# Splitting the weights of a hybrid decoder step: 40 tiles ahead of time and w_o in the tail

## The chip, the cores and the metric

The kernel runs on one core of a Trainium2 chip. The metric is the device time of one execution in microseconds (us). A core has five engines that matter here, each working through its own instructions in order: TensorE (PE, matrix products), VectorE (DVE), ScalarE (ACT), GpSimd (POOL) and SyncE (SP, which here only issues transfers). A DMA transfer stands in the line of the engine that issues it: SP for what the code calls `load`, ACT for `store_`. If it has to wait for data or for a buffer, what stands behind it in that line waits too. SBUF is the core's working memory, PSUM the small memory that PE writes to (banks of 512 numbers for each of 128 partitions).

## The reference

One inference step of a decoder layer, for a prompt of 1024 rows and 64 sample rows, together T = 1088 rows of 1024 numbers, all in float32. In short:

```python
h = rmsnorm(x, norm_g) * (1 + scale) + shift              # from a small product of c
u_pool, z_pool, z_ssm, xbc, dt_raw, g_raw = split(h @ w_in)
p = (pool_mix(u_pool) * silu(z_pool)) @ w_pool_out        # 512 -> 1024
xbc = silu(causal_conv(xbc))                              # four taps
y = ssd(x, dt, A, B, C, state) + d_skip * x               # chunks of 128 rows, 32 heads
s = rmsnorm(y * silu(z_ssm), ssm_norm_g) @ w_ssm_out      # 2048 -> 1024
m = sigmoid(g_pool) * p + sigmoid(g_ssm) * s
x = x + gate * (m @ w_o)                                  # 1024 -> 1024, then a last rmsnorm
```

The layer also gives back new states of pooling, convolution and SSD.

## The kernel before

**Products in three parts.** PE multiplies numbers of reduced precision (`float32r`) at its fast rate. So each operand is split: `hi` is the operand rounded to float32r by a copy on ACT, `lo` the rest, `operand - hi`, by a subtraction on POOL or DVE. A product is hi x hi + hi x lo + lo x hi, three matmuls (lines 332 to 334 in `gemm_`, 492 to 494 in `product`). `split` (L160) does this for the tiles of w_in when they are needed: copy L163, subtraction L164.

**The main part** (some 90 to 660 us) is the projection h @ w_in. Its columns are taken in pairs of 128; a pair is one Strassen step of seven products (`strassen`, L498), each of two column blocks (24 matmuls). `run_units` (L1156) goes through a list of 22 such pairs, ones with a convolution or pooling behind them ("heavy") mixed with ones that only apply an activation (L559) and store ("light"), and two `gate_unit`s. At every `yield` of a pair it calls `beside()`, which here is one step of the generator `splits()`: seven steps per pair, one per gate unit, 156 in all. A convolution (`conv_unit`, L683) makes its four taps at L711 and L713, the activation at L716 and L717; it also copies 27 columns together (t27, L701) that PE transposes at L704 for the new state. `u_unit` (L594) does the same for the pooling state (u64, L615; PE at L618).

**`splits`** (L378) makes the hi and lo tiles of the other three weight matrices and puts them in DRAM, from where later parts load them. A job is a tile of 128 x 4 x 128: 8 of w_pool_out (to `wp_d`), 32 of w_ssm_out (to `ws_d`, each multiplied first by the norm's gain, four copies at L392), 16 of w_o (to `wo_d`). Each job loads to `pw` (L388, SP), yields, copies to `ph` (L394, ACT), subtracts in place (L396, POOL, every third job DVE), yields, stores both parts (L398 and L399, SP), and yields again in three jobs out of four. `pw` and `ph` have one buffer each, so that a load waits for the store before it. When the list is through, what is left of `splits` is run out in one go (L1223) and `to_ssd` (L1194) gives the memory to the next part and starts `dt_end` (L759).

**The samples** (to some 935 us). `dt_end` loads the raw dt from DRAM (L772 and L773, SP), transposes it on PE (L786), works out dt and the cumulated decays on DVE (L787 to L811) and so on. Beside nine more light pairs run the states of the sample rows (`ssd_samples`, L898).

**The chunks** (`chunk`, L1063) are the SSD over 8 chunks for 4 groups of heads, with the products of w_pool_out (`P_unit`) and of three groups of w_ssm_out (`S_unit`) between them in an order written out by hand for PE (`in_line`, L1146; the loop at L1335). A chunk's second step makes exponentials on ACT: cE (L1073), POOL masks (L868), eight heads (L877). `p_split` (L1128) loads the pooled rows (L1133), copies them to hi (L1137, ACT) and subtracts (L1138, DVE); P_unit needs them.

**The tail.** `tail_unit(m)` (L1427) multiplies with the last group of w_ssm_out; `m_done` (L1408) loads the stored gate (L1410) and the pooling part (L1413), multiplies the gate by 1/rms on POOL (L1411) and has DVE add, multiply, add (L1418, L1423, L1424); `m_split` (L1390) splits the result (L1404 ACT, L1405 DVE). `wo_prep` (L1381) loads hi and lo of a row block of w_o from `wo_d` (L1386 and L1387), for the samples' products (L1399) and the last product (L1515 to L1517).

**What sets the order.** The kernel is written as one stream of instructions; a scheduler with a timeline model of its own then orders the instructions of each engine, by their place in the stream as priority and by when it thinks that they can start. `tc.issue_after(i)` adds a compile-time edge: what the block traces on i's engine comes behind i on that engine. The line numbers below are those of the profile.

Of the kernel before, what the change touches and what calls it, by code (L numbers as in the profile page):

```python
# [8 lines left out]
F32 = mybir.dt.float32  # L9
# [21 lines left out]
P = 128  # L31
# [25 lines left out]
def tile_pool_ssd_step(  # L57
# [314 lines left out]

    wp_d = [dram(f"wp{m}", [P, 2, 4, P]) for m in range(8)]
    ws_d = [[dram(f"ws{g}{m}", [P, 2, 4, P]) for m in range(8)] for g in range(NG)]
    wo_d = [dram(f"wo{k}", [P, 2, D]) for k in range(8)]


    def splits():  # L378
        jobs = [(w_pool_out[0, :, m * P:(m + 1) * P].rearrange("(k p) c -> p k c", p=P), None, wp_d[m])
                for m in range(8)]  # L380
        jobs += [(w_ssm_out[0, g * 512:(g + 1) * 512, m * P:(m + 1) * P].rearrange("(k p) c -> p k c", p=P),
                  24 + 4 * g, ws_d[g][m]) for g in range(NG) for m in range(8)]
        jobs += [(w_o[0, k * P:(k + 1) * P, c * 512:c * 512 + 512].rearrange("p (k c) -> p k c", k=4), None,
                  wo_d[k][:, :, c * 512:c * 512 + 512].rearrange("p s (k c) -> p s k c", k=4))
                 for k in range(8) for c in range(2)]
        for n, (src, gain, dst) in enumerate(jobs):
            raw = small([P, 4, P], "pw", 1)
            load(raw, src)  # L388
            yield
            if gain is not None:  # L390
                for k in range(4):
                    act(raw[:, k], raw[:, k], AF.Copy, scale=vT[:, gain + k:gain + k + 1])  # L392
            hi = gas[0].tile([P, 4, P], F32R, tag="ph", name=nm("ph"), bufs=1)
            act(hi, raw, AF.Copy)  # L394
            lo = raw.bitcast(F32R)
            (V if n % 3 == 2 else nc.gpsimd).tensor_tensor(lo, raw, hi.bitcast(F32), ALU.subtract)  # L396
            yield
            load(dst[:, 0], hi.bitcast(F32))  # L398
            load(dst[:, 1], raw)  # L399
            if n % 4 < 3:  # L400
                yield

    def ready(d):
        def ws():
            with tc.high_priority(PRI):
                hi, lo = [wp.tile([P, 4, P], F32R, tag=t, name=nm(t), bufs=4) for t in ("whi", "wlo")]
# [187 lines left out]
    def u_unit(gi):  # L594
# [20 lines left out]
        nc.gpsimd.tensor_copy(u64, us[:, :, 15:23])  # L615
        ps = PB()
        nc.tensor.transpose(ps[:15, :P], up[:, SEQ:SEQ + 15], ident)
        nc.tensor.transpose(ps[:NS, P:2 * P], u64.rearrange("p b t -> p (b t)"), ident)  # L618
# [64 lines left out]
    def conv_unit(mc, dst):  # L683
# [17 lines left out]
        nc.gpsimd.tensor_copy(t27.rearrange("p (s t) -> p s t", t=3),  # L701
                              rp[:, SEQ:SEQ + 99].rearrange("p (s t) -> p s t", t=11)[:, :, 0:3])
        ps = PB()
        nc.tensor.transpose(ps[:27, :P], t27, ident)  # L704
        o27 = sm.tile([27, P], F32, tag="o27", name=nm("o27"))
# [22 lines left out]
    def gate_unit(half):  # L728
        c = slice(2 * D + half * 512, 2 * D + half * 512 + 512)

        def ws():
            out = []
            for j in range(4):
                w = GA([P, 2, 512])
                load(w, w_ada[0, 2 * j * P:(2 * j + 2) * P, c].rearrange("(k p) c -> p k c", p=P))
                out.append(w)
            return out

        def run(w):
            bg = gas[0].tile([P, 512], F32, tag="ph", name=nm("bg"), bufs=1)[:NB + 1]  # L740
            load(bg, b_ada[0, c].partition_broadcast(NB + 1))
            pg = PB()
            for kk in range(2):
                for r in range(4):
                    k = 4 * kk + r
                    mm(pg[32 * r:32 * r + 32, :], scT[:, k, :], w[k // 2][:, k % 2], start=(kk == 0), stop=(kk == 1))
            gs = pa.tile([P, 512], F32, tag="c2", name=nm("gs"))
            act(gs, pg, AF.Copy)
            yield
            ps = PB()  # L750
            mm(ps[:NB + 1, :], sel9, gs, start=True, stop=True)
# [376 lines left out]
    def p_split():  # L1128
        ph, pl = Y4(hs), Y4(hs)
        ph_.extend(ph[:, gi] for gi in range(4))  # L1130
        pl_.extend(pl[:, gi] for gi in range(4))
        for gi in range(4):
            load(pl[:, gi].bitcast(F32), yp_d[:, gi])  # L1133
        yield
        for gi in range(4):
            y = pl[:, gi].bitcast(F32)
            act(ph[:, gi], y, AF.Copy)  # L1137
            V.tensor_tensor(pl[:, gi], y, ph[:, gi].bitcast(F32), ALU.subtract)  # L1138
        yield
    ph_, pl_ = [], []  # L1140
    p_in = p_split()
# [191 lines left out]
            made += 1  # L1333

    in_line(True)  # L1335
    for i in (0, 1, 0):
        next(seq[i])
    for i in range(len(seq)):
        if i + 1 < len(seq):
            next(seq[i + 1])  # L1340
# [228 lines left out]
```

## Time and profile before

| | us |
|---|---|
| median of 3 runs (lowest, highest) | 1443.96 (1440.91, 1443.97) |
| the profiled execution | 1441.96 |
| its span, first to last instruction | 1440.2 |
| busy: PE, weight load (PEld) | 1299.5, 1182.2 |
| busy: DVE, ACT, POOL | 878.9, 704.4, 721.8 |
| mean granted clock of PE, share of full | 0.951 |

The profile is of one execution. A row of a group names line, engine, operation, output tile <- inputs and shape, then busy time and mean (ns), and the idle time of the engine just before, with what ended it. A row of waits reads "engine, what it ran next <- what ended the wait: us in total, times, longest". A row of a timeline is start, duration, engine, line and instruction; SPq and ACTq rows are issues of transfers. A row of stretches is start:end, length, busy time (and instructions) of PE, PEld, DVE, ACT and POOL, granted clock, share of the DMA engines' time, GB/s.

### The profile page before, as it was taken

To read this page: it belongs to the slowest core of one execution; us is meant where nothing else is said; L and a number is where in the kernel's file an instruction comes from. 1 tells how busy PE (TensorE), PEld (TensorE's weight loads), DVE (VectorE), ACT (ScalarE), POOL (GpSimd) and SP (SyncE) were. 2 spreads that over 40 slices of the span, in tenths; PEclk is the share of its full clock that TensorE was granted. 3 is DMA by queue.
4 is the path that set the end of the run, shared out by engine and by line. 5 is a ranking of instruction groups with operands and counts; after the bars stand their busy time and mean duration, and the time that the engine had idled before them with its cause. 6 is when DMAs were issued, how large, how long until landed. Compare 5 with 4: busy or idle time off the path is not lost. (4 is left out here: it accounts for less than half of the span.)

```text
span 1440.2 us, 26096 instructions
## 1 busy us (share of the span) xinstructions
PE 1299.5 (90%) x9545; PEld 1182.2 (82%) x9545; DVE 878.9 (61%) x1443; ACT 704.4 (49%) x1615; POOL 721.8 (50%) x629
## 2 busy tenths in 40 slices
PE   5898999889799898893699999969999999999998
PEld 2778899789799898893688889958888888998886
DVE  2875666465665673882456656537766677659543
ACT  3753355355454453442365455485678776501111
POOL 2375476576666674773345345314556564724000
PEclk8899999999899999997699999979999999999999
DMA  9235456454445445454355555477886665466431
GB/s 372 78 102 166 159 187 220 130 160 159 136 150 170 135 144 187 159 170 163 97 154 143 172 166 171 150 271 253 273 281 189 193 191 173 142 252 205 182 113 73
DMA packets 230522, 251.68 MB, mean 175 GB/s; under 512 B 31101, under 2 KB 173573, under 8 KB 230386
## 3 DMA queue, kind: packets, MB, share of 16 engines
q1 hardware_dynamic: 187444, 196.73, 42.6%
q10 hardware_dynamic: 42950, 53.28, 10.9%
q8 instruction: 76, 1.25, 0.4%
q14 instruction: 52, 0.43, 0.1%
HBM read 167.06 MB, written 83.01 MB: 174 GB/s over the span
## 5 line engine op out<-in xcount | busy, mean ns | idle before, releaser
L164 POOL TENSOR_TENSOR wlo<-raw,whi 128x512 fp32r<-128x512 f32 x128 | 195.9, 1535 | 180.3 <-ACT whi L163 162.0
L164 POOL TENSOR_TENSOR wlo<-rawA,whi 128x512 fp32r<-128x512 f32 x93 | 142.6, 1537 | 115.9 <-ACT whi L163 105.8
L332 PE MATMUL mm<-Y,whi 128*128 128x352 f32 (+3 forms) x504 | 174.1, 347 | 16.2 <-ACT Y L1137 10.4
L333 PE MATMUL mm<-Y,whi 128*128 128x352 f32 (+3 forms) x504 | 167.8, 333 | 4.2 <-DVE Y L281 2.3
L334 PE MATMUL mm<-Y,wlo 128*128 128x352 f32 (+3 forms) x504 | 166.4, 330 | 0.0
L492 PE MATMUL ps<-Y,whi 128*128 128x272 f32 x496 | 152.2, 307 | 2.9 <-ACT o L706 1.8
L492 PE MATMUL mm<-Y,whi 128*128 128x272 f32 x496 | 147.7, 298 | 3.2 <-ACT whi L163 3.2
L493 PE MATMUL ps<-Y,whi 128*128 128x272 f32 x496 | 149.1, 301 | 0.0
L494 PE MATMUL mm<-Y,wlo 128*128 128x272 f32 x496 | 146.8, 296 | 2.6 <-POOL wlo L164 2.6
L494 PE MATMUL ps<-Y,wlo 128*128 128x272 f32 x496 | 148.7, 300 | 0.0
L493 PE MATMUL mm<-Y,whi 128*128 128x272 f32 x496 | 145.4, 293 | 1.4 <-DVE Y L431 1.4
L713 DVE SCALAR_TENSOR_TENSOR GA<-GA,cvT,GA 128x1112 f32<-128x1112 f32 x72 | 129.4, 1812 | 27.5 <-ACT GA L711 27.5
L332 PEld LDWEIGHTS mm<-Y,whi 128*128 128x128 f32 x504 | 96.0, 191 | 25.5 <-ACT Y L1137 11.6
L163 ACT ACTIVATE whi<-raw 128x512 fp32r<-128x512 f32 x128 | 79.2, 622 | 67.0 <-PE ps L493 54.0
L492 PEld LDWEIGHTS ps<-Y,whi 128*128 128x128 f32 x496 | 99.7, 201 | 5.7 <-ACT o L706 2.0
L333 PEld LDWEIGHTS mm<-Y,whi 128*128 128x128 f32 x504 | 96.6, 192 | 7.3 <-DVE Y L1138 3.6
L492 PEld LDWEIGHTS mm<-Y,whi 128*128 128x128 f32 x496 | 95.4, 192 | 8.3 <-ACT whi L163 4.1
L392 ACT ACTIVATE pw<-pw,vT 128x128 f32<-128x128 f32 x128 | 41.1, 391 | 120.1 <-DMA pw<-in_w_ssm_out 108.9
L493 PEld LDWEIGHTS ps<-Y,whi 128*128 128x128 f32 x496 | 99.7, 201 | 0.0
L494 PEld LDWEIGHTS ps<-Y,wlo 128*128 128x128 f32 x496 | 99.6, 201 | 0.0
L494 PEld LDWEIGHTS mm<-Y,wlo 128*128 128x128 f32 x496 | 95.6, 193 | 4.1 <-POOL wlo L164 3.9
L493 PEld LDWEIGHTS mm<-Y,whi 128*128 128x128 f32 x496 | 95.6, 193 | 2.3 <-DVE Y L431 1.9
(406 smaller groups left out, 3804.9 us busy)
## 6 DMA issues: line engine op xcount, KB each, us to landing
rawA<-in_w_in SPq DMA_DIRECT2D x46, 512.0 KB
dec<-acs_d SPq DMA_DIRECT2D x32, 512.0 KB
xbc<-GA ACTq DMA_DIRECT2D x24, 512.0 KB
xb<-xbc SPq DMA_DIRECT2D x32, 384.0 KB
rawA<-in_w_in SPq DMA_DIRECT2D x32, 256.0 KB
pw<-in_w_ssm_out SPq DMA_DIRECT2D x32, 256.0 KB
ws<-ph SPq DMA_DIRECT2D x32, 256.0 KB
ws<-pw SPq DMA_DIRECT2D x32, 256.0 KB
```

The lines of the kernel that those rows point to most:

```text
L163: act(hi[:, :, :ncols], raw[:, :, :ncols], AF.Copy)
L164: nc.gpsimd.tensor_tensor(lo[:, :, :ncols], raw[:, :, :ncols], hi[:, :, :ncols].bitcast(F32), ALU.subtract)
L332: mm(ps[:, :n], a, rh[k][:, o:o + n], start=(k == 0), stop=False)
L333: mm(ps[:, :n], a, rl[k][:, o:o + n], start=False, stop=False)
L334: mm(ps[:, :n], b, rh[k][:, o:o + n], start=False, stop=(k == nk - 1))
L392: act(raw[:, k], raw[:, k], AF.Copy, scale=vT[:, gain + k:gain + k + 1])
L492: mm(p, hi, ah, start=(k == 0), stop=False)
L493: mm(p, hi, al, start=False, stop=False)
L494: mm(p, lo, ah, start=False, stop=(k == 3))
L713: V.scalar_tensor_tensor(d[:, :n], rp[:, k:k + n], cvT[:, 24 * k + mc:24 * k + mc + 1], d[:, :n], ALU.mult, ALU.add)
```

## The change

- `splits` keeps 40 jobs; the 16 of w_o and the tensors `wo_d` go.
- A job's steps are spread: load; one step, or two in three jobs of four; gain, copy and the store of hi; a step later the store of lo; another step. The stores are issued by ACT, not SP. The block with ACT's instructions is traced under `behind(Activation)`: they come behind the last ACT instruction traced so far. All subtractions are POOL's.
- `wo_prep` loads w_o itself, copies to hi on ACT and subtracts on POOL, tile by tile in the tail.
- t27 and u64 are copied by ACT, not POOL. Two of the four subtractions of `p_split` go to POOL. `gate_unit` takes a buffer of the large kind.
- Ahead of the chunk loop the exponential steps of the first two chunks come behind the last ACT instruction traced so far.

```diff
-    wo_d = [dram(f"wo{k}", [P, 2, D]) for k in range(8)]
+    def behind(engine):
+        return tc.issue_after(next(i for i in reversed(nc.cur_bb.bb.instructions) if i.engine == engine))
...
-        jobs += [(w_o[0, k * P:(k + 1) * P, c * 512:c * 512 + 512].rearrange("p (k c) -> p k c", k=4), None,
-                  wo_d[k][:, :, c * 512:c * 512 + 512].rearrange("p s (k c) -> p s k c", k=4))
-                 for k in range(8) for c in range(2)]
         for n, (src, gain, dst) in enumerate(jobs):
-            raw = small([P, 4, P], "pw", 1)
-            load(raw, src)
+            raw = gas[0].tile([P, 4, P], F32, tag="pw", name=nm("pw"), bufs=1)
+            load(raw, src.rearrange("(k p) c -> p k c", p=P))
             yield
-            if gain is not None:
-                for k in range(4):
-                    act(raw[:, k], raw[:, k], AF.Copy, scale=vT[:, gain + k:gain + k + 1])
+            if n % 4:
+                yield
             hi = gas[0].tile([P, 4, P], F32R, tag="ph", name=nm("ph"), bufs=1)
-            act(hi, raw, AF.Copy)
-            lo = raw.bitcast(F32R)
-            (V if n % 3 == 2 else nc.gpsimd).tensor_tensor(lo, raw, hi.bitcast(F32), ALU.subtract)
+            with behind(mybir.EngineType.Activation):
+                if gain is not None:
+                    for k in range(4):
+                        act(raw[:, k], raw[:, k], AF.Copy, scale=vT[:, gain + k:gain + k + 1])
+                act(hi, raw, AF.Copy)
+                store_(dst[:, 0], hi.bitcast(F32))
+            nc.gpsimd.tensor_tensor(raw.bitcast(F32R), raw, hi.bitcast(F32), ALU.subtract)
             yield
-            load(dst[:, 0], hi.bitcast(F32))
-            load(dst[:, 1], raw)
-            if n % 4 < 3:
-                yield
+            with behind(mybir.EngineType.Activation):
+                store_(dst[:, 1], raw)
+            yield
...
-        nc.gpsimd.tensor_copy(u64, us[:, :, 15:23])
+        act(u64, us[:, :, 15:23], AF.Copy)
...
-        nc.gpsimd.tensor_copy(t27.rearrange("p (s t) -> p s t", t=3),
-                              rp[:, SEQ:SEQ + 99].rearrange("p (s t) -> p s t", t=11)[:, :, 0:3])
+        act(t27.rearrange("p (s t) -> p s t", t=3),
+                              rp[:, SEQ:SEQ + 99].rearrange("p (s t) -> p s t", t=11)[:, :, 0:3], AF.Copy)
...
-            bg = gas[0].tile([P, 512], F32, tag="ph", name=nm("bg"), bufs=1)[:NB + 1]
+            bg = GA([P, 512])[:NB + 1]
...
-            V.tensor_tensor(pl[:, gi], y, ph[:, gi].bitcast(F32), ALU.subtract)
+            (nc.gpsimd if gi % 2 else V).tensor_tensor(pl[:, gi], y, ph[:, gi].bitcast(F32), ALU.subtract)
...
-    for i in (0, 1, 0):
-        next(seq[i])
+    with behind(mybir.EngineType.Activation):
+        for i in (0, 1):
+            next(seq[i])
+    next(seq[0])
...
-        load(hi.bitcast(F32), wo_d[k][:, 0])
-        load(lo.bitcast(F32), wo_d[k][:, 1])
+        raw = M((P, D))
+        load(raw, w_o[0, k * P:(k + 1) * P, :])
+        act(hi, raw, AF.Copy)
+        nc.gpsimd.tensor_tensor(lo, raw, hi.bitcast(F32), ALU.subtract)
         wo[k] = (hi, lo)
```

More of the change, by code (lines that the diff above doesn't have):

```diff
@@ L374, in tile_pool_ssd_step @@
     ws_d = [[dram(f"ws{g}{m}", [P, 2, 4, P]) for m in range(8)] for g in range(NG)]
-    wo_d = [dram(f"wo{k}", [P, 2, D]) for k in range(8)]
+    def behind(engine):
+        return tc.issue_after(next(i for i in reversed(nc.cur_bb.bb.instructions) if i.engine == engine))
     def splits():
[L379 to L382, printed above, removed]
-        jobs += [(w_o[0, k * P:(k + 1) * P, c * 512:c * 512 + 512].rearrange("p (k c) -> p k c", k=4), None,
-                  wo_d[k][:, :, c * 512:c * 512 + 512].rearrange("p s (k c) -> p s k c", k=4))
-                 for k in range(8) for c in range(2)]
+        jobs = [(w_pool_out[0, :, m * P:(m + 1) * P], None, wp_d[m]) for m in range(8)]
+        jobs += [(w_ssm_out[0, g * 512:(g + 1) * 512, m * P:(m + 1) * P], 24 + 4 * g, ws_d[g][m])
+                 for g in range(NG) for m in range(8)]
@@ L403, in ready, with wtiles @@
+            nc.gpsimd.tensor_tensor(raw.bitcast(F32R), raw, hi.bitcast(F32), ALU.subtract)
+            yield
+            with behind(mybir.EngineType.Activation):
+                store_(dst[:, 1], raw)
+            yield
+    def wtiles():
+        return [wp.tile([P, 4, P], F32R, tag=t, name=nm(t), bufs=4) for t in ("whi", "wlo")]
     def ready(d):
@@ L405, in ws @@
             with tc.high_priority(PRI):
-                hi, lo = [wp.tile([P, 4, P], F32R, tag=t, name=nm(t), bufs=4) for t in ("whi", "wlo")]
+                hi, lo = wtiles()
                 load(hi.bitcast(F32), d[:, 0])
```

## The prediction

> **What bounds the kernel now.** I read the page first, for where TensorE (PE) is not busy.
>
> ```profile
> span 1440.2 us, 26096 instructions
> ...
> PE   5898999889799898893699999969999999999998
> ...
> ACT  3753355355454453442365455485678776501111
> ...
> PEclk8899999999899999997699999979999999999999
> ```
>
> Each digit is 36 us. PE is nearly full from slice 27 (972 us) on, and there are two holes before it: slices 18 and 19 (the seam from the projection to the sample states, here the first seam) and slice 26 (the seam to the chunks, the second). The stretches say how full PE is after the second seam and in the tail:
>
> ```profile
> 972.00:1260.00 288.00, 284.80 (x2266) 252.86 (x2265) 200.33 (x279) 198.38 (x546) 160.49 (x192) 0.99 0.67 212
> 1260.00:1332.00 72.00, 67.60 (x386) 63.60 (x385) 52.59 (x59) 7.73 (x13) 24.21 (x10) 1.00 0.67 229
> ```
>
> The columns are length, then busy time of PE, weight load, DVE, ACT, POOL, then clock. With PE busy 284.8 of 288 us, a microsecond that PE gains ahead of 972 us reaches the end. So the list of what PE waited for is a list of prices:
>
> ```profile
> PE ps L786 <- DMA s<-dts_d: 30.2, 1, 30.2
> ...
> PE ps L704 <- POOL t L701: 15.9, 6, 5.1
> ...
> PE mm L332 <- ACT Y L1137: 10.4, 3, 5.9
> ...
> PE ps L618 <- POOL u L615: 6.2, 2, 4.8
> ...
> PE mm L333 <- DVE Y L1138: 1.9, 3, 0.6
> ```
>
> Total, number and longest of the waits. The change touches all five. The longest of them begins at 693.25 - 30.19 = 663.06 us by PE's timeline:
>
> ```profile
> 693.25 1.12 PE L786 MATMUL ps<-ident,s 128*128 128x128 f32 x4 [30.19 <-DMA s<-dts_d]
> ```
>
> **The first seam, a wait removed.** Twelve-microsecond stretches around the 30.2 us:
>
> ```profile
> 648.00:660.00 12.00, 10.92 (x85) 10.48 (x84) 5.29 (x10) 6.41 (x15) 8.93 (x7) 1.00 0.77 266
> 660.00:672.00 12.00, 1.74 (x12) 1.55 (x12) 2.34 (x6) 1.90 (x4) 1.39 (x2) 0.71 0.26 98
> 672.00:684.00 12.00, 0.00 (x0) 0.00 (x0) 0.89 (x4) 0.63 (x1) 1.26 (x1) 0.50 0.36 126
> 684.00:696.00 12.00, 2.75 (x13) 2.76 (x14) 1.54 (x4) 0.63 (x1) 3.96 (x13) 0.50 0.37 114
> 696.00:708.00 12.00, 12.00 (x87) 11.95 (x87) 9.39 (x17) 7.19 (x12) 6.47 (x5) 0.87 0.34 106
> 708.00:720.00 12.00, 9.08 (x43) 7.64 (x41) 5.60 (x16) 5.26 (x9) 1.85 (x2) 0.72 0.23 72
> ```
>
> No engine is busy there: it is a chain of latencies. SyncE's (SP's) timeline shows which:
>
> ```profile
> 682.20 0.33 SPq L388 DMA_DIRECT2D pw<-in_w_o  x1
> ...
> 685.62 0.32 SPq L398 DMA_DIRECT2D wo<-ph  x1
> ...
> 686.96 0.32 SPq L399 DMA_DIRECT2D wo<-pw  x1
> ...
> 689.44 0.32 SPq L772 DMA_DIRECT2D s<-dts_d  x1
> ```
>
> This is the last split of w_o: load, copy, subtract, two stores, one buffer, so that each takes some 7 us end to end (682.20 to 689.44). The load of dt that PE's transposes of L786 need stands behind it on SP and issues 2.5 us after its last store. Leftover splits run one by one between 664 and 689 us. How late the splits are is in the rows of their tile:
>
> ```profile
> L388 SPq DMA_DIRECT2D pw<-in_w_ssm_out x32: 367/383/396, 186.5 to 539.4; - x32
> ...
> L388 SPq DMA_DIRECT2D pw<-in_w_o x16: 328/333/341, 556.0 to 682.2; - x16
> ...
> L388 SPq DMA_DIRECT2D pw<-in_w_pool_out x8: 383/390/498, 89.5 to 160.0; - x8
> ```
>
> The main part gives 22 pairs x 7 + 2 = 156 steps from 89.5 to about 663 us, 3.7 us each. 56 jobs of 2.75 steps ask for a job every 10.1 us; the middle row makes one each (539.4 - 186.5) / 31 = 11.4 us. So they fall behind and the rest spills over. After the change 40 jobs of 3.75 steps take 150 steps: 13.8 us each, above the 11.4 that the chain needs, and the last one ends near 89.5 + 150 x 3.7 = 645 us, some 18 us before PE's last product. The 16 jobs of w_o are gone. What is late next is dt's load itself, 3.8 us from issue (689.44) to PE's start (693.25), which can now run beside the last products. I take 28 of the 30.2 us; the ends are 0 (splits still late) and 30.2.
>
> The clock was 0.50 in the hole and 0.87 and 0.72 in the 24 us behind it: 12.0 x 0.13 + 9.08 x 0.28 = 4.1 us of PE work at most. In part PE waits there for the dt arithmetic anyway (9.08 of 12 busy), so I take 2 us.
>
> **The second seam, an order changed.** ScalarE's (ACT's) timeline with one row of the chain that ended last, and then two rows of the tail, for the price of such a subtraction on POOL (the group of L1411) and on DVE:
>
> ```profile
> 650.84 0.43 ACT L559 ACTIVATE u<-u 128x272 f32<-128x272 f32 x1 [0.40 <-ACT s L559]
> ...
> 939.95 10.50 DMA Y<-yp
> ...
> 949.13 1.28 ACT L1073 ACT_TABLE_LOAD   x1
> ...
> 956.89 1.09 ACT L1137 ACTIVATE Y<-Y 128x1088 fp32r<-128x1088 f32 x1
> ...
> 961.03 2.15 ACT L877 ACTIVATE dec<-dec,acT 128x128 f32<-128x128 f32 x7
> ...
> 967.44 1.09 ACT L1137 ACTIVATE Y<-Y 128x1088 fp32r<-128x1088 f32 x1
> ...
> L1411 POOL TENSOR_TENSOR R<-R,sq_acc 128x1088 f32<-128x1088 f32 x8 | 22.2, 2787 | 52.5 <-issue 32.9 <-DMA R<-gs 13.4 <-DVE m L1405 5.0
> ...
> 1302.07 1.28 DVE L1423 TENSOR_TENSOR G<-G,R 128x1088 f32<-128x1088 f32 x1
> ```
>
> The pooled rows have landed at 950.4, but the four copies of L1137 run between 956.89 and 968.5, mixed with exponentials of the first two chunks and with the sigmoids of L559; each swap of function loads a table (1.28 us). The pins put the exponentials behind the last sigmoid traced: four copies (4.4 us) and about five sigmoids (0.43 each, 2.1) could then be done near 957 in place of 968.5. The exponentials that follow (one table, 16 of about 0.3, cE) take some 7 us, to 964, when they also end now. Against that, two of four subtractions of L1138 go to POOL, 2.8 us for such a tile where DVE takes 1.3. Of 10.4 + 1.9 = 12.3 us I take 8; ends 0 and 12.3.
>
> [...]
>
> **The main part, work moved.** POOL's copies of t27 and u64 go to ACT, the stores of the splits from SP to ACT, and all 40 subtractions to POOL (before, 38 there and 18 on DVE).
>
> ```profile
> L701 POOL COPY t<-GA 128x27 f32<-128x27 f32 x24 | 12.0, 530 | 0.0
> ...
> L396 DVE TENSOR_TENSOR pw<-pw,ph 128x512 fp32r<-128x512 f32 x18 | 19.6, 1091 | 50.9 <-ACT ph L394 50.9
> ...
> ACT pw L392 <- DMA pw<-in_w_ssm_out: 108.9, 24, 8.4
> ...
> ACT ph L394 <- DMA pw<-in_w_o: 56.3, 13, 7.2
> ...
> SPq L399 <- POOL pw L396: 53.2, 36, 7.4
> ```
>
> PE's 15.9 + 6.2 = 22.1 us are waits for small copies that stand behind subtractions on POOL. On ACT, too, each should be a copy of no more than the 0.53 us that it takes on POOL. ACT has its own stalls, 108.9 + 56.3 us for loads of splits: the first shrinks, since the copies now come one or two steps (3.7 to 7.4 us) after the load and are pinned there; the second goes. I take 14 of the 22.1; ends 0 and 22.1.
>
> What is added: 40 pairs of stores stand in ACT's line. A store of ACT's own result costs a gap of 0.40 us (the row of L559 above): 40 x 0.4 = 16 us. The second store waits for POOL: SP waited 53.2 us in 36 such cases, 1.5 us each and 7.4 at worst, which for 40 is 59 us. Behind it on ACT stand the copies into whi (POOL and then PE's weights wait for them), the copies of L516 (DVE and PSUM banks) and the activations of the convolution. But the store is traced one step of 3.7 us after the subtraction, so that only the long waits show. I take 6 us on PE's path; ends 0 and 75. DVE loses 19.6 us of work and POOL 12.0 less 2 subtractions; PE is not counted as gaining from it, ACT's and PE's own work being the cover. At nothing too: gate_unit's buffer, and the 16 MB less that go out and back for w_o (no row of PE's waits names them).
>
> **The tail, work added.** Per row block of w_o: one 512 KB load in place of two, a copy on ACT (about 1 us; ACT is busy 7.73 of 72 us) and a subtraction of 128x1024 on POOL (2.6 us, from the 2.79 of L1411 by its columns). POOL has the time; DVE hasn't, and is held up by it:
>
> ```profile
> 1307.09 2.83 POOL L1411 TENSOR_TENSOR R<-R,sq_acc 128x1088 f32<-128x1088 f32 x1 [6.59 <-DMA R<-gs]
> ...
> 1308.05 3.02 DVE L1423 TENSOR_TENSOR G<-G,R 128x1088 f32<-128x1088 f32 x1
> ```
>
> The same DVE instruction takes 1.28 us alone (the row at 1302.07 above) and 3.02 beside POOL: it ends 1.15 us after POOL does, so it hardly ran before. In the tail DVE leads (chain of L1418, L1423, L1424, L1405) and PE follows closely. Five subtractions inside the units at 3.02 - 1.28 = 1.74 us are 8.7; the last three come in line after the seventh unit (w_o's last buffers come free only then), 2.6 us each, of which PE's partial sums hide some: 3.3. I take 12. The lower end is 0 (some run in POOL's idle stretch ahead of the tail, up to 32.9 us long by the group's row), the upper 8 x 2.6 = 21, all on the path.
>
> [...]
>
> **Sum.** -28 - 2 - 8 - 14 + 6 + 12 = -34 us. The profiled execution took 1441.96 us (span 1440.2 and 1.8 around it): 1408. The median of the runs is 2.0 above that: 1410.
>
> **Rivals.**
> 1. *The tail locks DVE out in full* (21 in place of 12) and the small copies gain only half (-7): 1410 + 9 + 7 = 1426. For it, the rows of L1423; against it, POOL's idle time ahead of the tail.
> 2. *The splits are still late.* If a job takes over 13.8 us (ACT reaches a copy late, the store waits, the next load waits for the store), a few jobs spill over again and dt's load stays behind them: the 28 us stay and the time is 1438. For it, four waits per job across four engines; against it, the 11.4 us measured and 18 us of slack at the end.
> 3. *Slower: ACT becomes the jam.* ACT waits at the second store for POOL, and whi, L516 and the convolution wait behind it. The price at most 75 us, less the 6 taken: 1410 + 69 = 1479. It decides from 34 us on the path, 0.85 us per job. For it, SP's 53.2 us of just this wait, on a queue where less stood behind it; against it, ACT is busy some half of this part (mostly digits 3 to 5 on the page), the wait comes a step later, and 165 us of ACT's older stalls shrink.
> 4. *It doesn't do what it says*: the scheduler puts the leftover elsewhere on the path, and nothing changes: 1444.
>
> **Chances.** Forecast (1394 to 1424) 0.68, rival 1 0.12, rival 2 0.08, rival 3 0.09, rival 4 0.03. A measurement here tells about 0.2% (2.9 us) from no change. Faster 0.88, same 0.03, slower 0.09. Range 1394 to 1434: low by both seams and the copies in full with a cheap tail, high to between rivals 1 and 2.
>
> **What would show it.** The wait of L786 under 5 us and a clock near 1 from 660 to 720: the first seam right; over 20: rival 2. L1137's copies in one row ahead of L877's exponentials, PE's wait there under 5: the second. ACT's waits for POOL's pw over 30 us, and PE waiting for whi and L516: rival 3. L1423 and L1424 near 3 us beside POOL's new subtraction, and the stretch from 1290 to 1350 longer by over 15 us after shifting: rival 1. I would be wrong altogether if PE found as much to wait for between 100 and 660 us as it lost.

## The result, and the profile after

The changed kernel takes 1382.43 us (median of 4 runs, 1380.84 to 1384.85), the kernel before 1443.62 us beside it (4 runs, 1440.91 to 1443.97): a ratio of 0.958, interval 0.956 to 0.960. The forecast was 1410 us, its range 1394 to 1434. The profiled execution took 1383.51 us, its span is 1381.8.

Page of the kernel after, the same lines as of before; PE's hole at slices 18 and 19 (digits 3 and 6 before) is gone, the one of the second seam is still there (8 and 7 at slices 25 and 26, counted from 0):

```profile
span 1381.8 us, 25855 instructions
...
PE   5899899898899999998999999879999999988998
...
ACT  3854355455455555554644554367688766121311
PEclk9899999999999999999999999979999999999999
```

Lines move by about four: L786 is L790, L704 is L708, L618 is L622, L394 is L396. PE's waits after:

```profile
PE ps L708 <- ACT t L705: 11.3, 6, 4.2
...
PE ps L622 <- ACT u L619: 6.2, 3, 2.5
...
PE ps L790 <- DMA s<-dts_d: 4.3, 1, 4.3
```

The wait for dt fell from 30.2 to 4.3 us. But the small copies, forecast to give 14 of their 22.1 us, still cost 11.3 + 6.2 = 17.5: ACT's now, not POOL's. The time came from elsewhere, as a comparison at the same work shows. A pair is 168 matmuls, so the start of a pair is found by counting. Pairs are numbered from 0 in PE's order, so that the 22 of the main part are 0 to 21 and 22 is the first beside the samples; a stretch runs from the start of one pair to the start of the other:

| stretch of the same work | before | after | difference | forecast |
|---|---|---|---|---|
| pairs 1 to 22 | 541.3 | 510.4 | -30.9 | -14 + 6 |
| first seam (pair 22 to 23) | 63.5 | 32.9 | -30.6 | -28 - 2 |
| sample states (pair 23 to 30) | 214.6 | 213.0 | -1.6 | 0 |
| second seam (pair 30 to the first product of L1105, now L1109) | 46.4 | 43.0 | -3.4 | -8 |
| chunks | 304.4 | 305.8 | +1.4 | 0 |
| tail | 160.4 | 166.3 | +5.9 | +12 |

With 0.8 us ahead of pair 1 that is the difference of the two spans, 58.4 us. The first row is the miss. Its stretches in the kernel before, cut at pairs 12 and 16 (length, then busy time of PE, weight load, DVE, ACT, POOL, then clock):

```profile
109.70:399.20 289.50, 261.87 (x1933) 248.97 (x1931) 177.66 (x280) 133.47 (x298) 186.62 (x132) 0.95 0.51 165
399.20:498.60 99.40, 91.72 (x689) 89.08 (x689) 61.64 (x101) 51.29 (x119) 67.75 (x47) 0.97 0.47 151
498.60:651.00 152.40, 137.75 (x1034) 134.54 (x1033) 105.43 (x148) 69.22 (x148) 104.58 (x73) 0.96 0.50 166
sum 541.30, PE 491.34 PEld 472.59 DVE 344.73 ACT 253.99 POOL 358.95; mean PE 163.78 PEld 157.53 DVE 114.91 ACT 84.66 POOL 119.65
```

And in the kernel after:

```profile
110.50:389.70 279.20, 256.74 (x1932) 244.35 (x1930) 176.33 (x272) 129.44 (x290) 181.87 (x121) 0.97 0.50 158
389.70:482.90 93.20, 88.32 (x690) 86.38 (x690) 60.47 (x97) 49.65 (x117) 67.05 (x43) 1.00 0.48 152
482.90:620.90 138.00, 132.05 (x1033) 129.24 (x1032) 97.33 (x139) 75.19 (x172) 98.94 (x65) 1.00 0.46 151
sum 510.40, PE 477.11 PEld 459.97 DVE 334.13 ACT 254.28 POOL 347.85; mean PE 159.04 PEld 153.32 DVE 111.38 ACT 84.76 POOL 115.95
```

PE stood still for 541.3 - 491.3 = 50.0 us before and 33.3 after, 16.7 less; and the same products took 477.1 us of busy time in place of 491.3, 14.2 less, at a higher clock.

What ACT waits for says where to look. Before, beside the 108.9 and 56.3 us of the prediction, there is a row for the first eight jobs; the other two rows are of after:

```profile
ACT ph L394 <- DMA pw<-in_w_pool_out: 22.8, 5, 7.1
```

```profile
ACT pw L395 <- DMA pw<-in_w_ssm_out: 80.2, 23, 6.6
...
ACT ph L396 <- DMA pw<-in_w_pool_out: 8.5, 4, 3.8
```

So the time in which ACT stands at a split's load, with what it would do for PE behind it, fell from 188 us to 88.7. In the kernel before, part of it stood behind the rows that name POOL. This is PE's second longest wait for a small copy, in the lines of ACT, POOL and PE:

```profile
135.27 0.63 ACT L394 ACTIVATE ph<-pw 128x512 fp32r<-128x512 f32 x1 [7.14 <-DMA pw<-in_w_pool_out]
```

```profile
135.98 1.27 POOL L396 TENSOR_TENSOR pw<-pw,ph 128x512 fp32r<-128x512 f32 x1 [4.64 <-ACT ph L394]
```

```profile
137.48 0.42 PE L618 MATMUL ps<-ident,u 128*64 128x128 f32 x1 [4.84 <-POOL u L615]
```

PE waits for POOL's copy, which stands behind a subtraction of `splits`; the subtraction waits for ACT, and ACT for the load. In the three longest of these waits (5.12, 4.84 and 3.26 us, together 13.2 of the 22.1) POOL had stood idle for 4.3 to 4.7 us for a split's copy on ACT, and ACT for 5.8 to 7.1 us ahead of that copy, in two of the three for its load by name. In the other five POOL was at work on the lo tiles of w_in (L164).

One such case in the kernel after, on three engines, first ACT:

```profile
357.00 0.33 ACTq L401 DMA_DIRECT2D ws<-pw  x1
...
365.18 1.28 ACT L395 ACTIVATE pw<-pw,vT 128x128 f32<-128x128 f32 x4 [6.59 <-DMA pw<-in_w_ssm_out]
366.36 0.21 ACT L705 ACTIVATE t<-GA 128x27 f32<-128x27 f32 x1
```

then SP, then PE:

```profile
362.24 0.37 SPq L387 DMA_DIRECT2D pw<-in_w_ssm_out  x1
```

```profile
366.63 0.41 PE L708 MATMUL ps<-ident,t 128*27 128x128 f32 x1 [4.16 <-ACT t L705]
```

The second store of a split is issued at 357.00. The next load has the same buffer and is issued only at 362.24, when that store has landed; over all jobs SP stood 180.1 us for this:

```profile
SPq L387 <- DMA ws<-pw: 180.1, 29, 12.3
```

The load lands at 365.18; ACT, which came to the copy 6.59 us before that, goes on, does the small copy at 366.36, and PE, which has waited for 4.16 us, transposes it. The row of waits says "ACT t"; the cause is two transfers in one buffer.

### The profile page after: what moved, and what is told of

The parts are those of the page before. It is cut to its first block, busy times and chain, and to the rows that moved or that the text cites. A ratio compares the mean times of both kernels' runs of the same rounds, so it can differ in the third digit from the quotient of the medians.

```text
span 1381.8 us, 25855 instructions
## 1 busy us (share of the span) xinstructions
PE 1284.0 (93%) x9545; PEld 1171.3 (85%) x9545; DVE 874.7 (63%) x1423; ACT 696.6 (50%) x1625; POOL 733.1 (53%) x613
## 5 line engine op out<-in xcount | busy, mean ns | idle before, releaser
L164 POOL TENSOR_TENSOR wlo<-raw,whi 128x512 fp32r<-128x512 f32 x128 | 182.3, 1428 | 174.9 <-ACT whi L163 150.6
L164 POOL TENSOR_TENSOR wlo<-rawA,whi 128x512 fp32r<-128x512 f32 x93 | 142.2, 1532 | 99.6 <-ACT whi L163 93.5
L717 DVE SCALAR_TENSOR_TENSOR GA<-GA,cvT,GA 128x1112 f32<-128x1112 f32 x72 | 134.0, 1876 | 30.4 <-ACT GA L715 29.2
L496 PE MATMUL ps<-Y,whi 128*128 128x272 f32 x496 | 147.0, 296 | 2.0 <-ACT o L710 2.0
L498 PE MATMUL mm<-Y,wlo 128*128 128x272 f32 x496 | 145.7, 294 | 0.9 <-POOL wlo L164 0.8
L497 PE MATMUL ps<-Y,whi 128*128 128x272 f32 x496 | 144.2, 291 | 0.0
L498 PE MATMUL ps<-Y,wlo 128*128 128x272 f32 x496 | 143.6, 289 | 0.0
L496 PEld LDWEIGHTS ps<-Y,whi 128*128 128x128 f32 x496 | 94.9, 191 | 4.3 <-ACT o L710 2.3
L334 PEld LDWEIGHTS mm<-Y,wlo 128*128 128x128 f32 x504 | 97.8, 194 | 0.3
L498 PEld LDWEIGHTS mm<-Y,wlo 128*128 128x128 f32 x496 | 94.9, 191 | 1.9 <-POOL wlo L164 1.5
L497 PEld LDWEIGHTS ps<-Y,whi 128*128 128x128 f32 x496 | 94.7, 191 | 0.0
L498 PEld LDWEIGHTS ps<-Y,wlo 128*128 128x128 f32 x496 | 94.6, 191 | 0.0
```

The source lines that it names most:

```text
L164: nc.gpsimd.tensor_tensor(lo[:, :, :ncols], raw[:, :, :ncols], hi[:, :, :ncols].bitcast(F32), ALU.subtract)
L334: mm(ps[:, :n], b, rh[k][:, o:o + n], start=False, stop=(k == nk - 1))
L496: mm(p, hi, ah, start=(k == 0), stop=False)
L497: mm(p, hi, al, start=False, stop=False)
L498: mm(p, lo, ah, start=False, stop=(k == 3))
L717: V.scalar_tensor_tensor(d[:, :n], rp[:, k:k + n], cvT[:, 24 * k + mc:24 * k + mc + 1], d[:, :n], ALU.mult, ALU.add)
```

## The experiments

Theories for the main part, at first: **copies** (my step, only too small: t27 and u64 left POOL), **jobs** (16 fewer jobs crowd the engines less), **queue** (stores left SP), **DVE** (subtractions left it); after the first runs also **load** (all of it is ACT standing at loads). In each diff the changed lines stand against the kernel that the text names. The table holds the runs that bear on it. Idle is PE's in pairs 1 to 22; "at loads" is the time that ACT stood at the gains and copies of splits for a transfer, up to 700 us (any transfer, so 196 for the kernel before, where the rows above, the splits' own loads, make 188); "seam" is pair 22 to pair 23. A ratio is to the kernel before as it ran beside that run, with medians of 1441 to 1449 us, so the times of different rows can differ by several us for that alone. The first two rows are the traces above; "e" is a run.

| kernel | time, us | ratio, 95% | pairs 1-22 | idle | at loads | seam |
|---|---|---|---|---|---|---|
| before | 1443.6 | | 541.3 | 50.0 | 196 | 63.5 |
| after | 1382.4 | 0.958 (0.956-0.960) | 510.4 | 33.3 | 89 | 32.9 |
| e1 before, w_o in the tail | 1396.0 | 0.969 (0.965-0.972) | 523.4 | 39.1 | 149 | 28.7 |
| e6 before, copies on ACT | 1430.6 | 0.992 (0.989-0.995) | 522.7 | 38.3 | 181 | 66.5 |
| e19 before, pins | 1439.5 | 0.994 (0.991-0.996) | 529.2 | 48.4 | 217 | 72.6 |
| e14 before, two buffers | 1388.4 | 0.959 (0.957-0.961) | 523.7 | 38.5 | 117 | 30.0 |
| e18 e1 and two buffers | 1380.7 | 0.953 (0.950-0.956) | 509.9 | 29.8 | 87 | 30.0 |
| e8 after again | 1380.7 | 0.956 (0.953-0.959) | 509.2 | 31.2 | 89 | 33.0 |
| e10 after, steps of before | 1399.0 | 0.967 (0.963-0.971) | 529.1 | 44.1 | 123 | 30.7 |
| e4 after, no pins | 1388.1 | 0.957 (0.953-0.960) | 512.1 | 32.6 | 101 | 30.6 |
| e3 after, copies on POOL | 1375.9 | 0.954 (0.951-0.957) | 500.7 | 28.6 | 74 | 31.9 |
| e2 after, stores on SP | 1376.4 | 0.954 (0.951-0.957) | 504.5 | 26.4 | 82 | 33.4 |
| e9 after, both of these | 1383.3 | 0.957 (0.954-0.960) | 514.3 | 32.0 | 90 | 29.5 |
| e7 after, a third of the subtractions on DVE | 1382.1 | 0.956 (0.953-0.959) | 509.5 | 29.4 | 83 | 33.1 |
| e15 e10 and two buffers | 1361.4 | 0.940 (0.936-0.944) | 485.1 | 15.0 | 21 | 30.7 |
| e16 e9 and two buffers | 1351.7 | 0.933 (0.931-0.935) | 484.0 | 13.9 | 16 | 30.4 |
| **e12 after, two buffers** | **1352.5** | 0.933 (0.931-0.935) | 473.8 | 5.8 | 12 | 33.4 |

### One part alone in the kernel before: w_o's jobs, the copies, the pins

Run e1 (the tail's preparation as in the change):

```diff
-        jobs += [(w_o[0, k * P:(k + 1) * P, c * 512:c * 512 + 512].rearrange("p (k c) -> p k c", k=4), None, ...
```

> The kernel before with one part of the change: the 16 jobs of w_o leave the splits and w_o is split in the tail (one load, one copy on ACT, one subtraction on POOL per row block). Pacing, engines and queues of the 40 other jobs as before. Jobs theory (the main part gained because fewer split jobs crowd ACT, POOL, DVE and SP late in it): the first seam gives 30, pairs 1 to 22 give most of their 31, the tail costs 6: about 1444 - 30 - 25 + 6 = 1395 us, and pair 22 starts 20 us or more earlier than in the kernel before. Small-copy theory (my step, under-sized: it gained because t27 and u64 left POOL): pairs 1 to 22 stay within 8 us of the kernel before, so 1444 - 30 + 6 = 1420 us, 1412 at the least. Queue theory (it gained because the stores left SP): the same 1420.

1396.0 us. The seam gave 34.8 and the stop in front of dt's transposes fell to 1.1 us. Pairs 1 to 16 took 389.2 us (before: 388.9), pairs 17 to 22 134.2 in place of 152.4. So w_o's jobs, which run in that place, cost 18 us there, and the seam besides; the 16.5 us that the change gained in pairs 1 to 16 (388.9 to 372.4) are something else.

Run e6:

```diff
-        nc.gpsimd.tensor_copy(u64, us[:, :, 15:23])
+        act(u64, us[:, :, 15:23], AF.Copy)
```

and the same for t27.

> The kernel before with the copies of t27 and u64 on ACT and nothing else changed. Small-copy theory: pairs 1 to 22 gain about 31 us (idle 17 and clock 14), the first seam stays as it is unless the leftover splits hold it at the same time: between 1413 and 1444 - 14 = 1430 us. Jobs theory: the waits move from POOL to ACT, pairs 1 to 22 gain less than 8 us, and since the splits still run over, the seam eats part of that: 1436 to 1444 us. Queue theory: the same as the jobs theory.

1430.6 us. Pairs 1 to 22 gained 18.6 us, so the copies theory was right that far; yet the time fell by only 11, at the edge of what it allowed. The wait for dt tells a part of why, in this run and then in that with the pins alone (e19):

```profile
PE ps L786 <- DMA s<-dts_d: 34.5, 1, 34.5
```

```profile
PE ps L791 <- DMA s<-dts_d: 38.3, 1, 38.3
```

Before it was 30.2. The splits go at their own pace; a PE that comes sooner meets more of them at the seam. Run e19, `with behind(mybir.EngineType.Activation):` around gain and copy in the kernel before:

> The kernel before with the pins of a split's copies on ACT and nothing else. Pin theory: ACT's wait for the loads (109 + 56 us) falls, pairs 1 to 16 gain 8 us or more, the splits still run over: 1420 to 1436 us. Rival (pins are worth something only with the added steps, or nothing): 1438 to 1450 us.

1439.5 us, within the rival's bounds; but the kernel before took 1448.4 us beside it, and 0.994 of 1443.6 is 1435, within those of the pin theory. In the trace pairs 1 to 16 gained 13.3 us, which is what the pin theory asked; then pairs 17 to 22 lost 1.2 and the seam 9.1. And ACT stood longer at loads, not shorter (217 us): the sum of these stands is not a price by itself, it depends on what stands behind each.

### One part undone in the kernel after: copies, queue, steps, DVE, pins

Run e8, nothing altered:

> The changed kernel once more, unaltered, as the yardstick for its variants on the same chip: 1382 us (0.9581 of the kernel before), with pairs 1 to 16 in 372 us, pairs 16 to 22 in 138 us and the four stops of over 3 us in front of PE where its trace shows them. If it comes out near 1376 (0.954), then putting the copies back on POOL or the stores back on SP gained nothing, and their 5 us were a difference between chips.

1380.7 us, 0.956. Run e3, t27 and u64 copied by `nc.gpsimd.tensor_copy` again:

> The changed kernel with the copies of t27 and u64 back on POOL. Small-copy theory: pairs 1 to 22 lose what they gained, 1382 + 14 to 31 = 1396 to 1413 us. Jobs theory: PE's waits for t and u move to POOL and stay near 17 us, 1382 to 1388 us. Queue theory: no change, 1382.

1375.9 us: the copies theory is out by some 20 us. Run e2, both stores from SP, that of lo without its pin:

```diff
-                store_(dst[:, 0], hi.bitcast(F32))
+                load(dst[:, 0], hi.bitcast(F32))
```

> The changed kernel with both stores of every split issued from SP again (the second one no longer pinned on ACT). Queue theory: the second store waits for POOL on SP, the loads of whi and wlo stand behind it, PE waits for whi and wlo again (5 us in the kernel before) and loses clock with each stop: 1390 to 1405 us. Jobs theory: with 40 jobs, 3.75 steps apart, SP has room: 1380 to 1385. Rival that ACT's line is what costs now: it gets faster, 1376 to 1380.

1376.4 us: the queue theory is out. Both runs lie lower than e8, but their intervals overlap its own; run e9, with both edits, was to show whether there is a gain.

> The changed kernel with the copies of t27 and u64 back on POOL and the stores of the splits back on SP, so that of the change only the removal of w_o, the steps and pins of the copies, the subtractions all on POOL and the second seam are left. Jobs-and-steps theory (what gains is fewer jobs and a load that has landed when ACT comes to its copy; who does the small copies and stores is worth nothing or less): 1370 to 1380 us, no slower than the changed kernel. Small-copy theory: 1395 or more. Queue theory (SP must be free): 1390 or more.

1383.3 us, as e8. So neither move shows a gain in the changed kernel, and the 5 us are not a price of either. Run e10:

```diff
-            if n % 4:
-                yield
...
-            yield
+            if n % 4 < 3:
+                yield
```

> The changed kernel with the splits' steps as in the kernel before: 2.75 per job, copies one step behind their load, the job ending a step early three times in four times... that is, no extra step between load and copies, and no step behind the second store of every fourth job. Jobs-and-steps theory: ACT comes to its copies 3.7 us earlier, stands longer for the load of the split (80 us in the changed kernel becomes 105 or more) with what PE needs behind it: pairs 1 to 16 lose 8 to 16 us, 1390 to 1398 us. Jobs alone (the spacing is worth nothing by itself): the splits end near 500 us, 1378 to 1385 us.

1399.0 us: 18 us more than e8, a little over the upper end. Its waits, ACT's and then PE's:

```profile
ACT pw L393 <- DMA pw<-in_w_ssm_out: 106.7, 29, 6.7
ACT ph L394 <- DMA pw<-in_w_pool_out: 16.7, 5, 4.4
```

```profile
PE ps L707 <- ACT t L704: 14.4, 5, 5.0
...
PE ps L621 <- ACT u L618: 5.8, 4, 3.4
```

One step of 3.7 us more per job, to which the prediction gave no price on PE, is worth 15.6 of these us in pairs 1 to 16 (386.8 us against 371.2 in e8), where the change had gained 16.5: of the parts undone one at a time it is the only one with a price. Three quarters of it lie between load and copies, one quarter at the end of a job, and a job is also asked for every 13.8 us in place of 10.1 (the prediction's estimate); e10 does not tell the distance from the pace. Nor do the parts add up: e10 keeps copies and pins, each of which gained 13 to 15 us in these pairs alone in the kernel before (e6, e19), and has next to nothing of it. Run e7, `(V if n % 3 == 2 else nc.gpsimd)` for the subtraction:

> The changed kernel with every third subtraction of a split on DVE again (13 of 40, 1.1 us each). DVE theory (part of the main part's gain came from DVE being freed, since PE waits for u and the sums of DVE): pairs 1 to 16 lose 5 to 15 us, 1387 to 1397 us. Jobs-and-steps theory: DVE loses 14 us of room and POOL gains it, no difference: 1380 to 1384 us.

1382.1 us: the DVE theory is out. Run e4, both `with behind(...)` of `splits` gone:

> The changed kernel without the pins that keep a split's copies and stores behind the ACT instructions traced before them; steps, engines and queues as changed. Pin theory (without them the scheduler puts the copies of a split far ahead in ACT's line, where their load has not landed, and what PE needs stands behind): ACT's wait for the load grows from 80 us to over 100, pairs 1 to 22 lose 10 to 25 us: 1392 to 1407 us. Rival (the steps alone set when ACT comes to the copies): 1378 to 1385 us.

Median 1388.1, ratio 0.957: no difference from e8 by the ratio, and 3 us in pairs 1 to 22. With the steps the pins add little.

### The buffer of the load

Run e12, the kernel after with

```diff
-            raw = gas[0].tile([P, 4, P], F32, tag="pw", name=nm("pw"), bufs=1)
+            raw = gas[0].tile([P, 4, P], F32, tag="pw", name=nm("pw"), bufs=2)
```

and the four small buffers of the tag "stc" made three for room:

> The changed kernel with two buffers instead of one for the split being loaded (one of four small buffers of another tile makes the room). The load of a split then no longer waits for the second store of the split before it. Load theory (what is left of PE's waits for t and u stands behind ACT's waits for the split's load): ACT's wait for that load falls from 80 us to under 30, PE's waits for t and u from 17 us to under 10, and the time to 1366 to 1376 us. Rival (these waits come from ACT's other work): ACT's wait moves to another instruction, 1380 to 1384 us.

1352.5 us, 0.933 (0.931 to 0.935) of the kernel before: below both kernels and below what was expected. ACT's and PE's waits:

```profile
ACT pw L395 <- DMA pw<-in_w_ssm_out: 5.3, 2, 2.7
```

```profile
PE ps L708 <- ACT t L705: 0.5, 1, 0.5
PE ps L622 <- ACT u L619: 0.3, 1, 0.3
```

and the stretches:

```profile
110.30:363.80 253.50, 248.84 (x1931) 238.45 (x1929) 177.75 (x272) 132.82 (x298) 182.62 (x121) 1.00 0.55 177
363.80:453.00 89.20, 88.36 (x690) 86.46 (x690) 61.70 (x98) 49.68 (x114) 66.42 (x46) 1.00 0.51 163
453.00:584.10 131.10, 130.82 (x1033) 129.03 (x1033) 101.24 (x144) 73.72 (x168) 94.71 (x62) 1.00 0.46 149
```

PE waits 5.8 us in 474, the clock is at 1.00, and 17.5 us of "ACT t" and "ACT u" have become 0.8 with the same copies on the same engine. That shows the load as the cause of what the changed kernel had left. Is it the cause of all? Run e14, two buffers in the kernel before:

> The kernel before with two buffers for the split being loaded and nothing else of the change (room as in the other run with two buffers). Load theory (one cause): pairs 1 to 22 fall from 541 us to 475 to 490, the splits no longer fall behind, so that the wait of 30 us in front of the transposes of dt is gone as well: 1355 to 1370 us. Rival (several causes: number of jobs, small copies behind subtractions on POOL, stores on SP): ACT's wait for the load falls, but PE's waits for t and u on POOL (22 us) and the spill stay: 1395 to 1430 us.

1388.4 us: between the two, nearer to several causes. The seam gave 33.5 us, as the load theory has it, and pairs 17 to 22 13.3. Pairs 1 to 16 gave 4.3; PE still waits there for the copies on POOL:

```profile
PE ps L704 <- POOL t L701: 15.8, 7, 4.1
...
PE ps L618 <- POOL u L615: 6.8, 3, 3.7
```

My one cause falls for that half. Runs e15 (e10 with two buffers), e16 (e9 with two buffers) and e18 (e1 with two buffers):

> The changed kernel with two load buffers and the splits' steps as in the kernel before (2.75 per job, copies one step behind the load). Load theory: with the load landed early the extra steps are worth nothing: 1348 to 1358 us. Rival (the spacing is worth something of its own, the 18 us that it is worth with one buffer): 1362 to 1372 us.

> The changed kernel with two load buffers, the small copies on POOL and the split stores on SP. Load theory: ACT's and POOL's lines move freely, it matters little who copies: 1348 to 1358 us. Rival (the second store's wait for POOL on SP now holds the loads behind it, or copies behind subtractions on POOL hold PE): 1362 to 1380 us.

> The kernel before with two load buffers and w_o split in the tail; small copies, stores, steps, every third subtraction on DVE and the second seam as before. Load theory: as the changed kernel with two buffers, but for the second seam (8 us by the run with the old order): 1352 to 1364 us. Rival (the other edits have a part of their own): 1370 to 1395 us.

e15: 1361.4, between the two; the steps are worth 9 us with two buffers and 18 with one. e16: 1351.7, as e12; who copies and who stores stays without a price. e18: 1380.7, 28 us over e12, the rival. Between e18 and e15 lie 27 us in pairs 1 to 12 (289.1 and 262.0), with two buffers and 2.75 steps in both: pins, subtractions, copies, stores and the buffer of `gate_unit`, of which no run separates the shares.

### The clock

Run e11, in front of four waits in the kernel after, with n of 26 to 36:

```diff
+            for _ in range(n):
+                nc.tensor.transpose(ps[:, :P], ident, ident)
```

> The changed kernel with idle PE products of the identity with itself put ahead of four of its waits (28 before the first pooling product, 26 each before the transposes of the ninth and eleventh convolution, 36 before the transposes of dt), each about 0.12 us, into a bank that the waiting transpose overwrites. PE then works through most of the 3.6, 3.1, 3.2 and 4.9 us that it waits there. It leaves nothing out and removes no wait. Clock theory (a stop of PE of some 3 us lowers its granted clock for the 10 to 20 us behind it, so that a stop costs nearly twice its length): the clock behind these four places stays at 0.95 or more where it was 0.69 to 0.83, PE's busy time for the same products falls by 5 to 8 us and the time to 1373 to 1377 us. Rival (the clock follows something else, and stops cost their length alone): the clock dips stay, 1382 us or somewhat more.

1390.1 us, 0.960 (0.958 to 0.963): no gain. Around the first two places, in e8 and then in e11:

```profile
138.00:150.00 12.00, 8.40 (x46) 6.91 (x45) 7.75 (x17) 0.91 (x3) 3.53 (x3) 0.86 0.61 186
306.00:318.00 12.00, 8.89 (x53) 8.60 (x53) 4.40 (x9) 6.60 (x15) 7.71 (x6) 0.75 0.62 162
```

```profile
138.00:150.00 12.00, 10.80 (x82) 9.87 (x81) 8.86 (x18) 1.21 (x5) 4.56 (x4) 1.00 0.62 180
306.00:318.00 12.00, 9.46 (x78) 9.03 (x78) 4.42 (x9) 6.15 (x13) 7.74 (x6) 1.00 0.62 163
```

So at these two places the stop lowered the clock (0.86 and 0.75 over the 12 us), and a busy PE kept it at 1.00. But pairs 1 to 12 took 277.2 us (e8: 277.4), with 9.2 us of filler (80 products) in them: PE came sooner to waits of 2.8 us (at 284) and 3.3 us (at 396) that e8 does not have. The half of my theory that says "what the clock loses is lost time" fell for these stops: PE's time went into other waits for ACT and DVE. The some 10 us by which e11 is slower as a whole (6 by the ratios) lie in small amounts behind pair 12; that stays open.

### The tail and the second seam

Run e13, `act(lo, raw, AF.Copy)` for the subtraction on POOL in `wo_prep`, which leaves the low part of w_o out of the result:

> The changed kernel without the eight subtractions of w_o on POOL in the tail: the low part is a second copy on ACT instead, so the low part of w_o is left out of the computation (it holds the whole weight again) while loads and products are the same in number and size. As predicted, POOL's subtraction locks DVE out: the tail from the first unit falls from 166 us to 154, 1370 us. By the trace, the tail lost 5.8 us: 160 us, 1376. Rival (the tail is longer for other reasons, the load or the copy on ACT): no change, 1382.

1384.2 us, 0.955 (0.953 to 0.957), tail 165.6: no change. Why, ACT's timeline shows, of before and of after:

```profile
1252.82 1.28 ACT L1372 ACT_TABLE_LOAD   x1
1280.56 0.47 ACT L1372 ACTIVATE sq_acc<-ps,eps 128x256 f32<-128x256 f32 x1 [26.46 <-PE ps L1371]
```

```profile
1215.72 2.00 ACT L1394 ACTIVATE Y<-m 128x1024 fp32r<-128x1024 f32 x2 [27.16 <-PE mm L333]
1217.74 1.28 ACT L1378 ACT_TABLE_LOAD   x1
1219.04 1.47 ACT L1378 ACTIVATE sq_acc<-ps,eps 128x256 f32<-128x256 f32 x3
```

The square root, from which the tail starts, came 0.8 us after its first product (at 1279.8) before, its table loaded in idle time. Now two copies of w_o, which waited 27.16 us for their buffers, and then the table stand ahead of it: 3.5 us after the product (1215.5). That is 2.8 us more at the start of the tail, of the 5.9 in all, and PE then stops once for 3.5 us for DVE (at 1223.6). In e13 four copies stand there instead of two and the square root comes 5.4 us after the product, so what POOL gave, ACT took; the run does not price POOL's subtraction by itself. Rows of POOL and DVE do show the lock:

```profile
1235.18 3.39 POOL L1395 TENSOR_TENSOR Y<-m,Y 128x1024 fp32r<-128x1024 f32 x1
```

```profile
1236.69 1.97 DVE L1402 TENSOR_TENSOR sh<-G,sh 128x64 fp32r<-128x64 f32 x1 [0.32 <-ACT sh L1401]
...
1245.69 0.21 DVE L1402 TENSOR_TENSOR sh<-G,sh 128x64 fp32r<-128x64 f32 x1
```

Beside the new subtraction (L1395) a DVE instruction of 0.21 us takes 1.97 and ends just after it, at 1238.66 against 1238.57. Over the whole tail DVE is busy for 97.5 us before, 105.4 after and 98.8 in e13, where the subtraction is gone: POOL's work holds DVE for some 7 us. But only four of the eight subtractions meet a DVE instruction that they hold; three run ahead, beside nothing or DVE's reciprocals (0.89 us with or without them), and one later beside no work of DVE. How much of the 7 us reaches the end, no run shows.

Run e5:

```diff
-    with behind(mybir.EngineType.Activation):
-        for i in (0, 1):
-            next(seq[i])
-    next(seq[0])
+    for i in (0, 1, 0):
+        next(seq[i])
```

> The changed kernel with the order at the second seam as before: the exponentials of the first two chunks are no longer pinned behind the last sigmoid traced. By the trace the pins gave 2 us: the stretch from the last sample product to the steady chunks grows by 2 us, 1384. As predicted, they gave 8 and another edit took 6 back: that stretch grows by 8 us, 1390. Rival (the pins are worth nothing, or cost): 1376 to 1382.

1390.8 us, 0.961 (0.959 to 0.963). The stretch from pair 30 to the chunks is 48.6 us, 5.9 over e8's 42.7. The order gave 5.9, not 2; other edits took back 2.2 (48.6 against 46.4 in the kernel before). In the kernel after the first and the last of the copies of L1141 now lie 4.5 us apart, ahead of the exponentials:

```profile
890.87 1.11 ACT L1141 ACTIVATE Y<-Y 128x1088 fp32r<-128x1088 f32 x1 [3.35 <-DMA R<-gp]
...
895.35 1.09 ACT L1141 ACTIVATE Y<-Y 128x1088 fp32r<-128x1088 f32 x1
897.20 1.28 ACT L881 ACT_TABLE_LOAD   x1 [0.28 <-DMA whi<-wp]
```

## Why the prediction was wrong, point by point

- **First seam: right.** -30.6 us against -28 - 2, for the reason given (leftover splits ahead of dt's load): e1 and e14 remove it by either way, fewer jobs or a faster job.
- **Main part: the step that failed**, "I take 14 of the 22.1 ... I take 6 us on PE's path", -8 where -30.9 was measured. Its price list was PE's waits by the name of the releaser, and it took POOL's 22.1 us for waits "behind subtractions on POOL"; 13.2 of them are three waits that lead back to ACT, idle ahead of a split's copy. In the changed kernel these waits have only changed their name (17.5 us on ACT), and with the copies back on POOL no time is lost (e3). I had the rows of ACT's stands at loads (108.9 + 56.3; with w_pool_out 188, after the change 88.7) and wrote that "the first shrinks", "the second goes", without a price on PE. Two edits that I counted at nothing there had one: the added step (18 us, e10, most of it in pairs 1 to 16) and w_o's jobs in pairs 17 to 22 (18 us, e1). They overlap with copies and pins, each of which is worth 12 to 19 us in pairs 1 to 22 alone in the kernel before and shows no gain in the changed one; how the 30.9 us divide among the edits stays open.
- **The clock in the main part** had no term, though the first seam had one: 14.2 of the 30.9 us are busy time of the same products. It is no cause of its own: with the stops gone in e12 the loss is gone too (477.1 to 468.0), and holding the clock up at the first two of four stops (1.00 in place of 0.86 and 0.75) gave nothing over pairs 1 to 12 (277.2 us against 277.4, e11).
- **ACT's stores, +6:** no cost found at the steps of the changed kernel (e2, e9). Rival 3, ACT as the jam, did not come. ACT's line had been part of the jam already, in the kernel before (the three waits of 13.2 us), and the change eased it; it was not all of it, as e14 shows.
- **Second seam:** mechanism right, -5.9 for the order against -8 (e5), less 2.2 of other edits, of which e5 does not say which.
- **Tail:** +5.9 against +12. The lock of DVE is there (some 7 us of DVE's time), but 2.8 us of the cost are something else: copies of w_o and a table load ahead of the square root. What the lock itself cost stays open.

The sum of the steps other than the main part was -28 - 2 - 8 + 12 = -26; they measured -30.6 - 3.4 + 5.9 = -28.1, close in part by luck, since the second seam and the tail missed in opposite directions. The main part alone put the time outside the range; that range had taken a gain of the copies in full (22.1 us) as its end.

## What to carry to other kernels

A wait is priced by following the releaser's own line back: where an engine stands at a transfer ahead of what others need, its stall belongs on the list, whichever name the row has. Before moving work between engines, look whether the transfer that they stand at shares a buffer with the one before it; here a second buffer was worth another 28 us on top of the change (0.956 to 0.933 by the ratios, some 33 us), while the moves of copies and stores gained nothing in the changed kernel, with it or without it, though the copies alone had gained in the kernel before. When a background job falls behind the work that paces it, a gain ahead of its backlog is in part paid back at the backlog (34.5 and 38.3 us in place of 30.2).

## What the runs showed of the hardware

Half clock came here after a shorter stop than the some 3 us of my clock theory. In the kernel before, a stop of 1.9 us at 170.4 us, with PE at work again from its end on, is followed by this (2 us stretches):

```profile
170.00:172.00 2.00, 0.38 (x4) 0.16 (x2) 2.00 (x4) 2.00 (x3) 0.00 (x0) 1.00 0.25 100
172.00:174.00 2.00, 1.73 (x6) 0.84 (x7) 2.00 (x4) 0.54 (x3) 0.00 (x0) 0.88 0.45 178
174.00:176.00 2.00, 2.00 (x11) 2.00 (x10) 2.00 (x3) 0.00 (x0) 0.00 (x0) 0.50 0.22 64
176.00:178.00 2.00, 2.00 (x15) 2.00 (x14) 2.00 (x2) 0.97 (x3) 0.91 (x1) 0.76 0.05 9
```

while one of 1.7 us at 321.5 us leaves it at 1.00. Nor does the lowered clock last the 10 to 20 us of that theory: behind the stops that end at 145.7, 315.6, 366.6 and 628.5 us in the kernel after (3.60, 3.08, 4.16 and 4.35 us long) it is 0.50 and back at 1.00 from 152, 319, 370 and 637 us on. Over pairs 1 to 22 of before and of e12, 44.2 us less idle time (50.0 to 5.8) went with 23.3 us less busy time for the same products (491.3 to 468.0).
